# Re-timing a hand-planned instruction order: second mixer, stage openings, a fourth seven-product chunk

## The chip, the cores and the metric

One Trainium2 chip, one core. The metric is the device time of one execution in microseconds (us). The kernel before took 955.35 us (median of 3 runs, 955.19 to 955.69).

## The reference

A trunk of two layers on x (256 x 1024, float32). Each layer does

```
x = x + 0.5 * SwiGLU_1(rmsnorm(x))           # D_FF = 2816
h = rmsnorm(x); q_s|k_s|v_s|q_m = h @ W_in   # 1024 x 2560
self attention: layer 0 chunked with relative bias (12 heads),
                layer 1 differential with rotary, block-causal (6 heads)
memory attention: 4 heads into mem (256 x 1024)
x = x + concat(self, mem) @ W_out
x = x + 0.5 * SwiGLU_2(rmsnorm(x))
```

The differential attention of layer 1 norms each head of q and k (a power of -1/2), turns them by the rotary tables, takes two softmaxes a pair of heads, subtracts the second times lambda, and norms the result again.

## The kernel before, in words

**Products in three passes.** Every float32 weight and activation is split into a high part and a rest (`hi`, `lo`, both in the matrix engine's float32 format). One product is three matmuls of 512 columns: high by high (L511), high activation by low weight (L514), low activation by high weight (L517), all issued by the helper `dense`. ScalarE makes the high part (`split_hi`, L338), VectorE the rest (`split_lo`, L356).

**Stages.** For each layer: gate/up of FFN 1, down of FFN 1, the mixer, gate/up of FFN 2, down of FFN 2. Gate/up runs over 11 column groups g of 256 with two halves c of the contraction; two neighbouring groups are done with seven products in place of eight (`PAIR`). Down runs over 11 row chunks of 256. An ordinary down chunk is eight products. A chunk listed in `SEVEN` is seven: four sums of weight blocks are made on VectorE (L350) and four sums of activations (`seven_forms`, L681 to L694), and seven splits of the weights are made in place of four. The first such chunk of a stage takes two weight buffers; each later one ("guest") takes one and the two buffers of x's transposes, `xh` and `xl`, which are free in a down stage; the flag `xt_room` hands them from one guest to the next after the last product of the former. The last three down chunks are done output block by output block.

**The way of h.** After a gate/up group, `evac` makes h, writes it to DRAM (`hd`, L650) and reads it back turned (`hr`, L656), 3 us and then 2 us later by the plan. Four `hd` buffers rotate. The reads, the writes and all weight loads (L294, three raw buffers) go through one in-order queue, that of SyncE (SP).

**The order is written out by a planner.** `Flow` keeps a clock of its own while the program is built. Every step is a generator; it issues an instruction, adds the planned duration to its engine's time, and is taken up again when that time has come. The matrix engine's stream is issued by the main loop (`flow.pe`), the rest in between. So planned durations set only the order in each engine's queue; on the chip each engine runs its queue in order and waits on semaphores. Planned: 0.216 us a matmul, VectorE 0.07 + n/960, ScalarE 0.15 + n/1200, GpSimd as written at each call. `rsqrt` (L528) does the power on GpSimd (L532) with a planned 0.3 + 0.165 n us. The rotary step in `qk_evac` has two multiplications on GpSimd (L1259, planned 1.4 us together), one on VectorE (L1262) and their sum (L1266), before the transposes to the heads' layout (`qktp`, L525). In `attn_diff` the probabilities are transposed (`ptp`), multiplied with V (L1498), normed (L1512, L1514) and transposed again (`otp`).

**Stage openings.** `prep_half` transposes half of x's columns for one block of 128 rows, scales it (L557), makes `xh` on ScalarE (L560) and `xl` on VectorE (L562). Group 0 of every gate/up stage but the first goes row block by row block (`plain_chunk(0, c, (tb,))`), so that the first block's products run while the second block is prepared. `dense` waits for `xl` before its first pass.

## Time and profile before

| what | us |
|---|---|
| median of 3 runs | 955.35 |
| the profiled execution | 955.69 |
| its span, first to last instruction | 953.9 |
| PE busy (matmul) | 945.6 |
| VectorE busy | 820.0 |
| ScalarE busy | 587.0 |
| GpSimd busy | 109.1 |

In the profile PE is the matmul engine, DVE VectorE, ACT ScalarE, POOL GpSimd, SP SyncE; L and a number is a line of the kernel. Matmuls overlap in a pipeline, so that each shows a longer duration than the step from its start to the next one's start; it is the step that counts for the stream.

### The profile page before, as it was taken

Reading aid. Unit: us, or ns where it says so; the run is one execution under the profiler, and the core shown is the slowest. Engines: PE = TensorE matmul, PEld = TensorE weight load, DVE = VectorE, ACT = ScalarE, POOL = GpSimd, SP = SyncE. Lnnn points to the kernel's source line nnn. Section 1 sums busy time; section 2 is a strip of 40 time slices with the busy share of each in tenths; the row PEclk is TensorE's granted clock in tenths of the full one; section 3 lists DMA queues with packets and bytes.
Section 4 is the critical chain, followed back from the end, with each engine's and each line's share of the span. In section 5 each row is a group of like instructions: output and inputs, shape, how many; then the busy total and the mean of one; then the engine's idle time right before and its main releaser. Section 6 shows DMA issues by size and latency. Waiting matters only on the chain.

```text
span 953.9 us, 13334 instructions
## 1 busy us (share of the span) xinstructions
PE 945.6 (99%) x4475; PEld 774.1 (81%) x4475; DVE 820.0 (86%) x1483; ACT 587.0 (62%) x1121; POOL 109.1 (11%) x160
## 2 busy tenths in 40 slices
PE   9999999999999999999999999999999999999998
PEld 7888888887777888888888888888787778888886
DVE  7898978888777899979889899796999888999884
ACT  6556566677676746647546656564676865665650
POOL 1000057621210100000000000000434200000000
PEclk9999999999999999999999999999999999999999
DMA  8987799486525387887746679775641367588751
GB/s 265 289 263 236 224 354 296 158 276 210 177 90 177 97 266 225 262 287 219 245 146 219 208 226 288 247 253 166 196 158 57 121 214 228 183 275 276 239 197 45
DMA packets 169887, 204.04 MB, mean 214 GB/s; under 512 B 10137, under 2 KB 145114, under 8 KB 169818
## 3 DMA queue, kind: packets, MB, share of 16 engines
q1 hardware_dynamic: 169498, 202.78, 66.0%
q8 instruction: 35, 0.57, 0.3%
q10 hardware_dynamic: 320, 0.40, 0.1%
q14 instruction: 34, 0.28, 0.1%
HBM read 188.99 MB, written 14.16 MB: 213 GB/s over the span
## 4 chain that ended last, share of the span: by engine, by line
PE 90%; DVE 6%; DMA 2%; ACT 1%; issue 1%; SPq 0%; ACTq 0%; DVEq 0%
PE gu L517 13%; PE gu L514 13%; PE gu L511 13%; PE acc L511 9%; PE acc L517 9%; PE acc L514 9%; PE pair_m L511 3%; PE pair_m L514 3%; PE pair_m L517 3%; PE pj L517 2%; PE pj L511 2%; PE pj L514 2%; DVE lo L356 2%; PE S L1360 1%; DMA x<-in_x_dram 1%; PE AV L1441 1%
## 5 line engine op out<-in xcount | busy, mean ns | idle before, releaser
L338 ACT CAST hi<-raw 128x512 fp32r<-128x512 f32 (+1 forms) x467 | 336.3, 770 | 172.6 <-DMA raw<-in_ffn_w_up_dram 45.6
L356 DVE TENSOR_TENSOR lo<-raw,hi 128x512 fp32r<-128x512 f32 (+1 forms) x467 | 391.9, 875 | 35.5 <-ACT hi L338 35.4
L514 PE MATMUL gu<-lo,xh 128*128 128x512 f32 x576 | 224.7, 390 | 0.5 <-DVE lo L356 0.5
L517 PE MATMUL gu<-hi,xl 128*128 128x512 f32 x576 | 224.5, 390 | 0.4 <-DVE xl L562 0.4
L511 PE MATMUL gu<-hi,xh 128*128 128x512 f32 x576 | 224.4, 390 | 0.0
L517 PEld LDWEIGHTS gu<-hi,xl 128*128 128x128 f32 x576 | 108.1, 188 | 23.9 <-DVE xl L562 1.7
L514 PEld LDWEIGHTS gu<-lo,xh 128*128 128x128 f32 x576 | 108.1, 188 | 23.5 <-DVE lo L356 1.4
L511 PEld LDWEIGHTS gu<-hi,xh 128*128 128x128 f32 x576 | 108.2, 188 | 22.3
L517 PE MATMUL acc<-hi,ht 128*128 128x512 f32 x280 | 109.5, 391 | 0.0
L511 PE MATMUL acc<-hi,ht 128*128 128x512 f32 x280 | 109.2, 390 | 0.0
L514 PE MATMUL acc<-lo,ht 128*128 128x512 f32 x280 | 109.1, 390 | 0.0
L338 ACT CAST hi<-wsum 128x512 fp32r<-128x512 f32 x82 | 47.7, 619 | 26.5 <-DVE wsum L350 26.5
L514 PE MATMUL pj<-lo,xh 128*128 128x512 f32 x160 | 64.0, 400 | 0.0
L517 PE MATMUL pj<-hi,xl 128*128 128x512 f32 x160 | 63.8, 399 | 0.0
L511 PE MATMUL pj<-hi,xh 128*128 128x512 f32 x160 | 63.8, 399 | 0.0
L514 PEld LDWEIGHTS acc<-lo,ht 128*128 128x128 f32 x280 | 52.6, 188 | 10.9
L517 PEld LDWEIGHTS acc<-hi,ht 128*128 128x128 f32 x280 | 52.6, 188 | 10.8
L511 PEld LDWEIGHTS acc<-hi,ht 128*128 128x128 f32 x280 | 52.6, 188 | 10.7
L532 POOL TENSOR_TENSOR xr<-v,nhalf 128x1 f32<-128x1 f32 x12 | 10.3, 861 | 435.1 <-DVE v L530 435.1
L356 DVE TENSOR_TENSOR lo<-wsum,hi 128x512 fp32r<-128x512 f32 x82 | 52.8, 680 | 0.0
L633 ACT ACTIVATE sil<-gu,xr 128x256 f32<-128x256 f32 x72 | 33.7, 468 | 29.8 <-PE gu L517 29.7
L532 POOL TENSOR_TENSOR hf<-v,nhalf 128x8 f32<-128x8 f32 (+1 forms) x20 | 31.4, 1570 | 87.3 <-DVE v L530 78.9
(232 smaller groups left out, 1429.5 us busy)
## 6 DMA issues: line engine op xcount, KB each, us to landing
raw<-in_ffn_w_down_dram SPq DMA_DIRECT2D x176, 256.0 KB, 4.5
raw<-in_ffn_w_gate_dram SPq DMA_DIRECT2D x82, 512.0 KB, 4.0
raw<-in_ffn_w_up_dram SPq DMA_DIRECT2D x82, 512.0 KB, 5.4
raw<-in_w_in_dram SPq DMA_DIRECT2D x32, 512.0 KB, 4.4
hd<-hb SPq DMA_DIRECT2D x44, 256.0 KB, 4.6
hr<-hd SPq DMA_DIRECT2D x44, 256.0 KB, 4.6
raw<-in_w_out_dram SPq DMA_DIRECT2D x8, 1024.0 KB, 5.1
raw<-in_w_mem_kv_dram SPq DMA_DIRECT2D x4, 1024.0 KB, 5.3
```

The source lines that it names most:

```text
L338: nc.scalar.copy(out=it.part(0, q, w), in_=src())
L356: nc.vector.tensor_sub(it.part(1, q, w), src(), it.part(0, q, w).bitcast(F32))
L511: nc.tensor.matmul(out=ps, lhsT=xh, rhs=wh, start=start, stop=False)
L514: nc.tensor.matmul(out=ps, lhsT=xh, rhs=wl, start=False, stop=False)
L517: nc.tensor.matmul(out=ps, lhsT=xl, rhs=wh, start=False, stop=stop)
L532: nc.gpsimd.tensor_tensor(out=dst, in0=v[:, :n], in1=nhalf[:, :n], op=ALU.pow)
L633: nc.scalar.activation(sil, ps[tb][:, 0:256], AF.Silu, scale=xt.r[tb])
L1360: nc.tensor.matmul(out=ss[e][:, pr, :nk], lhsT=q[rows, pr, :], rhs=k[rows, pr, :], start=i == 0, stop=i == len(passes) - 1)
L1441: nc.tensor.matmul(out=av[64 * e:64 * e + 64, pr, :], lhsT=vsrc(kb, pr, e), rhs=pts[e][:, pr, kb, :], start=(kb == 0), stop=(kb == nb - 1))
```

## The change

The list of seven-product down chunks of the last stage goes from (1, 4, 7) to (1, 3, 5, 7). A new helper `two_phases` takes the place of `dense` where group 0 is done row block by row block: for four slices it issues the two passes with `xh`, then the four passes with `xl`; it waits first for the time of `xh` (kept in the new list `th`) and only then for that of `xl`. The planned time of the power on GpSimd becomes 0.5 + 0.17 n, that of the rotary multiplications 2.1. In `attn_diff` two steps are resumed 0.3 us later. The reading of h is issued 8 us in place of 2 us after the write's buffer is given back, for all groups but the last three.

```
-    SEVEN = {(0, 1): (), (0, 2): (1, 4, 7), (1, 1): (1, 4, 7), (1, 2): (1, 4, 7)}
+    SEVEN = {(0, 1): (), (0, 2): (1, 4, 7), (1, 1): (1, 4, 7), (1, 2): (1, 3, 5, 7)}
...
         nc.tensor.matmul(out=ps, lhsT=xl, rhs=wh, start=False, stop=stop)
+        used(c)
+        return flow.pe(T_MM)
+
+    def used(c):
         c.uses -= 1
         if c.uses == 0:
             hl_left[0] += c.n
             xt_room[0] |= c.guest
-        return flow.pe(T_MM)
+
+    def two_phases(ps, xt, tb, c, kks, start, stop):
+
+        for k, kk in enumerate(kks):
+            flow.until(lambda: c.lot[k] is not None and xt.th[tb][kk] is not None)
+            flow.at(max(xt.th[tb][kk], c.lot[k]))
+            at[0] = max(at[0], c.index)
+            for i, w in enumerate((c.part(0, k), c.part(1, k))):
+                nc.tensor.matmul(out=ps, lhsT=xt.h[tb][:, kk, :], rhs=w, start=start and k == i == 0, stop=False)
+                flow.pe(T_MM)
+                flow.step()
+        for k, kk in enumerate(kks):
+            flow.until(lambda: xt.t[tb][kk] is not None)
+            flow.at(xt.t[tb][kk])
+            nc.tensor.matmul(out=ps, lhsT=xt.l[tb][:, kk, :], rhs=c.part(0, k), start=False, stop=stop and kk == kks[-1])
+            used(c)
+            t = flow.pe(T_MM)
+            flow.step()
+        return t
...
-        yield flow.pool(0.3 + 0.165 * n)
+        yield flow.pool(0.5 + 0.17 * n)
...
         nc.scalar.copy(out=xt.h[tb][:, ks, :], in_=y)
-        yield flow.act(512)
+        t = flow.act(512)
+        xt.th[tb][ks] = [t] * 4
+        yield t
...
             g2.give()
-            yield flow.now + 2.0
+            yield flow.now + (8.0 if g < NG - 3 else 2.0)
             yield g2.has()
...
             for tb in tbs:
+                if len(tbs) == 1:
+                    t = two_phases(ps[tb], xt, tb, plan[l, nm, "gu"][g, c], range(4 * c, 4 * c + 4), c == 0, c == 1)
+                    if c == 1:
+                        end[tb] = t
+                    continue
...
                     flow.dve(512)
-                    yield flow.pool(1.4)
+                    yield flow.pool(2.1)
                     nc.vector.tensor_add(m1, m1, m2)
...
             pt, t = yield from p_transpose(e0, nk)
-            yield t
+            yield t + 0.3
...
             t = flow.dve(256)
             banks.give()
-            yield t
+            yield t + 0.3
             yield from o_transpose(o, tb, grp, gcs[:, 3:4])
```

## Rows read from the trace of the kernel before

**Rows 1.** The page: busy time of each engine, its share of the span, instructions.
```profile
PE 945.6 (99%) x4475; PEld 774.1 (81%) x4475; DVE 820.0 (86%) x1483; ACT 587.0 (62%) x1121; POOL 109.1 (11%) x160
```

**Rows 2.** Waits of PE, whole span: who waited for whom, us, times, longest.
```profile
PE qktp L525 <- DVE m L1266: 0.7, 2, 0.6
PE otp L525 <- DVE of L1512: 0.5, 1, 0.5
...
PE AV L1498 <- ACT PT L1374: 0.5, 1, 0.5
PE gu L517 <- DVE xl L562: 0.4, 1, 0.4
```

**Rows 3.** Windows (stretch, length; PE, PEld, DVE, ACT, POOL busy; clock): mixers, last down.
```profile
222.00:305.00 83.00, 83.00 (x515) 65.14 (x516) 65.24 (x179) 60.75 (x158) 11.45 (x7) 1.00 0.48 154
...
680.00:750.00 70.00, 68.03 (x373) 53.40 (x372) 65.39 (x147) 49.28 (x140) 28.49 (x24) 1.00 0.41 136
...
892.00:950.00 58.00, 58.00 (x257) 47.88 (x255) 43.88 (x77) 26.20 (x51) 0.00 (x0) 1.00 0.46 150
```

**Rows 4.** Timeline of PE, second mixer: start, duration, [idle before, releaser].
```profile
679.75 0.39 PE L517 MATMUL pj<-hi,xl 128*128 128x512 f32 x1
...
685.19 0.39 PE L517 MATMUL pj<-hi,xl 128*128 128x512 f32 x1
686.15 0.63 PE L525 MATMUL qktp<-ident,m 128*128 128x128 f32 x4 [0.57 <-DVE m L1266]
...
726.49 0.71 PE L1498 MATMUL AV<-V,PT 128*128 128x128 f32 x4 [0.45 <-ACT PT L1374]
...
745.23 0.41 PE L525 MATMUL otp<-ident,o 128*128 128x128 f32 x2 [0.49 <-DVE of L1512]
```

**Rows 5.** Groups of VectorE and ScalarE, 880 to 953 us: count, busy, mean ns.
```profile
L350 DVE TENSOR_TENSOR wsum<-raw,wsum 128x512 f32<-128x512 f32 x6 | 4.1, 686 | 0.1
...
L338 ACT CAST hi<-wsum 128x512 fp32r<-128x512 f32 x6 | 3.5, 617 | 0.0
```

**Rows 6.** Timeline, last down stage: PE's first matmul, VectorE, a weight load on SP.
```profile
892.26 0.39 PE L511 MATMUL acc<-hi,ht 128*128 128x512 f32 x1
...
913.18 0.28 DVE L681 TENSOR_TENSOR sf<-hr 128x128 f32<-128x128 f32 x1
...
916.58 0.68 DVE L694 TENSOR_TENSOR h<-sf,h 128x512 fp32r<-128x512 f32 x1
...
922.00 4.93 DVE L356 TENSOR_TENSOR lo<-raw,hi 128x512 fp32r<-128x512 f32 x8
...
919.70 2.53 SPq L294 DMA_DIRECT2D raw<-in_ffn_w_down_dram  x4
```

**Rows 7.** The page, DMA issues: KB each and median us from issue to landing.
```profile
raw<-in_ffn_w_down_dram SPq DMA_DIRECT2D x176, 256.0 KB, 4.5
```

**Rows 8.** Timeline of VectorE and PE at the opening of the last gate/up stage.
```profile
783.08 0.65 DVE L562 TENSOR_TENSOR xl<-y,xh 128x512 fp32r<-128x512 f32 x1
...
783.04 0.39 PE L514 MATMUL gu<-lo,xh 128*128 128x512 f32 x1
783.78 0.50 PE L517 MATMUL gu<-hi,xl 128*128 128x512 f32 x1 [0.35 <-DVE xl L562]
```

**Rows 9.** Waits of the SP queue, whole span: us, times, longest.
```profile
SPq L656 <- DMA hd<-hb: 50.1, 22, 4.7
```

**Rows 10.** Groups of GpSimd by shape, 660 to 790 us: count, busy, mean ns.
```profile
L1259 POOL TENSOR_TENSOR m<-qkn,ropeS 128x256 f32<-128x256 f32 x12 | 12.1, 1027 | 7.5 <-DVE qkn L925 4.7 <-ACT k L1022 1.8 <-PE pj L517 1.1
L532 POOL TENSOR_TENSOR hf<-v,nhalf 128x8 f32<-128x8 f32 x6 | 11.0, 1832 | 17.4 <-DVE v L530 9.1 <-DVE sst L583 8.3
L532 POOL TENSOR_TENSOR of<-v,nhalf 128x2 f32<-128x2 f32 x6 | 6.3, 1056 | 24.4 <-DVE v L530 24.4
```

**Rows 11.** Timeline of VectorE and GpSimd around one rotary multiplication.
```profile
681.19 1.23 DVE L1262 TENSOR_TENSOR m<-qkn,ropeC 128x512 f32<-128x512 f32 x1
...
680.89 2.12 POOL L1259 TENSOR_TENSOR m<-qkn,ropeS 128x256 f32<-128x256 f32 x2 [1.08 <-PE pj L517]
```

More of the change, by code (lines that the diff above doesn't have):

```diff
@@ L541, in __init__ @@
             self.r = [sm.tile([P, 1], F32, tag="xr", name="xr", bufs=4) for _ in range(2)]
-            self.t = [[None] * KT for _ in range(2)]
+            self.t, self.th = ([[None] * KT for _ in range(2)] for _ in range(2))
             self.rt = [None, None]
```

## The prediction

> **What bounds the kernel.** I read the page first. PE is busy for 945.6 of 953.9 us [rows 1], at the full granted clock in every window read (1.00, the 2.4 GHz level, [rows 3]), so the matmul stream is the limit and only two things can change the time: fewer matmuls, or fewer holes in the stream. How large the holes are the busy share does not tell. Therefore the list of PE's waits came second [rows 2], the windows by stage third [rows 3], and the timeline at each hole last [rows 4]. Apart from the first 13 us, which the change leaves alone, the trace has holes in two places: the second mixer, where PE lacks 70.00 - 68.03 = 1.97 us between 680 and 750, and the opening of the last gate/up stage, where it waits 0.4 us for `xl`. Mixer 1 and the last down stage have none [rows 3].
>
> The reader should see what a hole really costs. In a full stream one matmul of 512 columns starts 0.227 us after the other: 24 steps from 679.75 to 685.19 are 5.44 us [rows 4]. The transpose at 686.15 starts 0.96 us after the matmul before it, 0.73 late, though the profile calls 0.57 of this idle. So each hole costs about 0.16 us above its idle time, since the overlap of neighbours is lost too. The mixer's idle time is spread over seven holes; the three largest are in the group, the other four share 1.97 - 1.51 = 0.46 us. The loss is 1.97 + 7 x 0.16 = 3.1 us.
>
> **The change, part by part.**
>
> *The fourth seven-product chunk.* The list goes from three entries to four, so one product, three matmuls, falls away: 3 x 0.227 = 0.68 us of the stream. What it adds lies beside the stream: four more weight sums (0.69 us alone, [rows 5]) and three more splits on VectorE, in a row some 0.61 us each (8 splits in 4.93 us, [rows 6]), 4.3 us; three more casts of 0.62 us on ScalarE, which is busy 26 of 58 us; and the activation sums with their splits, 2.3 us of VectorE (four at 0.2 us and 1.5 us of splits, the last of 0.68; the one chunk in the group spreads them from 913.18 to 917.3 between weight work). VectorE has 58.00 - 43.88 = 14.1 us to spare in this stage [rows 3], so these 6.6 us fit as a total. What matters is when. A guest's splits may begin only after the last product of the guest before it, and guests stand two chunks apart now, not three. With the down stage starting at 892.26 [rows 6] and 0.68 us a product, chunk 3 ends at 912.66; chunk 5 runs from 918.10 to 922.86, chunk 7 from 928.30 to 933.06. Chunk 5's seven splits are through at about 912.7 + 0.9 + 4.3 = 917.9 (0.9: the first cast and 0.3 for hand-overs), and its third product, which uses the seventh split, comes at 919.5. Chunk 7's are through at 922.9 + 0.9 + 4.3 = 928.1, needed at 929.7. The margin is 1.6 us both times. Chunk 10's load, issued at 919.70 now, waits for chunk 7's three plain splits, until about 925.5; 2.5 us of issuing and 4.5 us to the landing of a piece [rows 6, 7] make 932.5 at the latest; cast and split by 934; needed at 933.06 + 4 x 0.68 = 935.8. I take no stall: -0.68 us. Bounds: -0.68, and +2.3 if the activation sums of chunks 5 and 7 (4.6 us), which the plan lets begin at chunk 3, fall wholly into chunk 5's splits: its third product is then 3.0 us late.
>
> *The openings.* Group 0 waits for `xl` at 783.78, 0.74 us after the matmul before it, so 0.51 us late, with one step 0.11 too long behind it: 0.62 us [rows 8]. With the passes of `xh` first, six other matmuls, 1.4 us, come ahead of the first that needs `xl`, more than the 0.5 missing; `xh` was there in time before. -0.62 us. The two other openings have no hole and gain nothing; the count of matmuls and weight loads is the same. Next to be late would be `xh` itself, made one VectorE step earlier. Bounds -0.62 and 0.
>
> *h read later.* Nothing on PE waits for h or for a weight's landing [rows 2], so both signs are hidden. It spares SP up to 50.1 us of standing at a read whose write has not landed, 22 times, with weight loads queued behind it [rows 9]; those loads were not late for PE either. On the other side h comes 6 us later for groups 0 to 7; the latest of these, group 7, still has three gate/up groups of 48 matmuls (10.9 us each) before the down stage begins. If that cover were gone, a late chunk would cost its whole lateness. I take 0; bounds ±0.3, half of one hole.
>
> *Planned times.* They move no work, only places in the queues. A power of eight values is planned at 1.62 us and measures 1.83; the pair of rotary multiplications 1.4 against 2 x 1.03 = 2.06; the power of two values 0.63 against 1.06 [rows 10]. So the planner puts the sum (L1266) and the transposes behind it too early: VectorE and then PE stand at an instruction whose input is not there, and what is queued behind stands too, weight splits on VectorE and projection matmuls on PE. After the change the planned chain up to `qktp` is 0.24 + 0.7 = 0.94 us longer; the holes at `qktp` are all smaller (0.73 the largest). The chain to `otp` gains 0.3 + 0.2 + 0.3 = 0.8 against a hole of 0.65. `AV` gains 0.3 against 0.61 with its idle 0.45, so 0.3 stays; one hole at `ptp` after the softmax gets no margin of its own and I leave it, 0.3. For new holes that a shuffled order opens I take 0.3. Gain 3.1 - 0.3 - 0.3 - 0.3 = 2.2 us. Bounds: -3.1 (all gone) and 0. VectorE has 4.6 us free in that window [rows 3], enough. Mixer 1 gets the longer power as well; it has no holes, its VectorE is busy only 65 of 83 us [rows 3], and later planning loosens it: 0.
>
> The sum: -0.68 - 0.62 - 2.2 = -3.5 us. From the profiled execution's 955.69 that is 952.2; the median stands 0.34 below it, so **951.9 us**.
>
> **A rule against the fixed numbers.** In the trace the VectorE multiplication that runs beside GpSimd's two takes 1.23 us [rows 11], where a two-input subtraction of the same size takes 0.68 with GpSimd idle [rows 6]: they hold each other up by 0.55 us. So neither duration is a constant that a planner can know. The Trainium skill, page "SBUF — State Buffer", section "SBUF: two separate sides", says why: GpSimd shares a port pair with VectorE instructions that read two SBUF inputs, as "an exclusive lock, not a bandwidth split", and the loser waits out the whole instruction. The measured 0.55 fits such a lock. What the behaviour would make of the time is rival 1.
>
> **The rivals.**
> 1. *Half of the holes come back at other places.* The new order sets other VectorE instructions beside GpSimd's; each of the six rotary steps costs 0.55 us somewhere, 3.3 us in all, and the holes return in part. For it: [rows 11], and VectorE busy 93% of this window. Against it: the new 2.1 already holds the shared time (2.06). Mixer gain about 0.9: 955.35 - 0.68 - 0.62 - 0.9 = 953.1 us. Chance 0.22.
> 2. *The last stage pays.* Chunk 5 or 7 stalls by up to the bound, 3.0 us; say 2: 951.9 + 2 = 953.9. For it: margins of 1.6 us only. Against: PE runs 5% slower than planned (0.227 to 0.216) and VectorE as planned, so a place that is free in the plan is freer on the chip. Chance 0.10.
> 3. *Slower.* In the second mixer the gap that the longer rotary step opens in VectorE's plan is filled with a weight split (0.6 to 0.7 us), which on the chip runs late and stands before the sum that the transposes wait for. One such split at all six chains is 4.2 us, with the old holes kept: 955.35 - 1.3 + 4.2 = 958.2. From two chains on (1.4 us) it outweighs the other gains, and from five (3.5 us) the kernel is slower by over 0.2%. For it: VectorE's 93%. Against it: the planner puts a split only where it sees VectorE free. Chance 0.08.
> 4. *The re-planning does nothing on balance*, and only the dropped product and the opening show: 955.35 - 1.3 = 954.05. Chance 0.06.
>
> The forecast, 951.0 to 953.0, has 0.54.
>
> **How the numbers follow.** On the good side the bounds of the terms add to 955.35 - 4.4 = 950.9, with 0.3 for h 950.6. On the other side the range takes in rivals 1, 2 and 4 up to 954.8 and leaves out rival 3 and the worst of 2, some 0.12 together. 0.2% is 1.9 us, about what a measurement of this kernel can tell from no change; faster by more means under 953.44. That is all of the forecast, two thirds of rival 1 and a little of rival 2: 0.54 + 0.15 + 0.03 = 0.72. Slower by more is most of rival 3, 0.07. The rest, 0.21, is within.
>
> **What would show it.** In the changed kernel's trace PE's waits name no `xl`; PE's idle time in the second mixer's 70 us is below 0.8 in place of 1.97; the last down stage has 84 products in place of 85, 57.1 us, and no hole; L656 does not stand on `hd`. The prediction is wrong if PE waits for `lo` after 912 us (rival 2), if the mixer's holes remain under other names (rivals 1, 4) or grow behind L356 (rival 3).

## The result, and the profile after

The changed kernel takes **958.86 us** (median of 22 runs, 955.34 to 961.42) where the kernel before, run between them, takes 955.53 (22 runs, 954.45 to 956.77): a ratio of 1.0030, with a 95% interval of 1.0022 to 1.0039. It is slower by 3.3 us; the prediction said 951.9 and a range up to 954.8. **It was wrong, in sign and in size.**

The profiled run of the changed kernel took 961.42, the slowest of its 22, so its rows show 2.6 us more loss than the median has. In ten of the 22 runs the mean granted clock is 0.996 to 0.998 and the median time 960.3, in the other twelve it is 0.999 or 1.0 and the median 957.1. Stage by stage, from the first matmul of a stage to the first of the next in PE's timeline (us):

| stage | before | after | difference | predicted |
|---|---|---|---|---|
| to the first matmul | 7.13 | 7.30 | +0.17 | 0 |
| FFN 1 of layer 0, memory's K and V | 204.49 | 205.58 | +1.09 | 0 |
| mixer 1 | 103.65 | 103.32 | -0.33 | 0 |
| FFN 2 of layer 0, FFN 1 of layer 1 | 353.36 | 353.36 | 0 | 0 |
| mixer 2, projections | 70.95 | 68.49 | -2.46 | -2.2 for |
| mixer 2, output products | 34.60 | 40.45 | **+5.85** | the mixer |
| last gate/up | 118.08 | 117.43 | -0.65 | -0.62 |
| last down | 57.57 | 59.30 | **+1.73** | -0.68 |
| last matmul to the span's end | 4.07 | 4.38 | +0.31 | 0 |

The sum is 5.71, the difference of the spans (959.6 - 953.9). Two gains look right almost to the digit, and two stages lose what nobody priced. Of the -2.46 some 0.2 is only moved: two transposes more, at steps of 0.11 us, come behind the first output product (362 instructions of PE stand before it in the kernel before, 360 after). How much of the rest is gain is worked out below. The 1.09 is mostly the landing of x at the start, which varies from run to run (PE waits 0.3 us for x in the profile before and 1.3 here).

The page's busy line of the changed kernel answers to [rows 1]: three matmuls fewer, thirteen VectorE instructions more, and PE "busy" 2.2 us longer.

```profile
PE 947.8 (99%) x4472; PEld 776.0 (81%) x4472; DVE 825.1 (86%) x1496; ACT 589.9 (61%) x1126; POOL 108.0 (11%) x160
```

Fewer matmuls that are busy for longer: the windows below show a stretch at the lower clock, which the busy share hides. PE's waits over the whole span [rows 2] name new waits, and `xl` no longer:

```profile
PE S L1389 <- ACT PT L1403: 2.0, 2, 1.8
PE acc L514 <- DVE lo L356: 1.8, 2, 1.0
...
PE qktp L547 <- DVE m L1295: 0.2, 1, 0.2
```

The windows of [rows 3], same stretches and columns:

```profile
222.00:305.00 83.00, 82.99 (x512) 65.53 (x511) 65.50 (x180) 62.34 (x160) 11.46 (x7) 1.00 0.48 155
680.00:750.00 70.00, 69.41 (x381) 54.86 (x379) 65.35 (x147) 49.72 (x141) 27.79 (x25) 1.00 0.42 133
892.00:950.00 58.00, 56.17 (x247) 45.89 (x246) 52.96 (x99) 32.96 (x64) 0.00 (x0) 1.00 0.49 159
```

In the second mixer's first 70 us PE now lacks 0.59 us in place of 1.97. The last down stage, which had no hole, lacks 1.83, and VectorE works 9.1 us more there (8.4 when both windows are laid from the stage's first matmul; in e1 below, with the fourth chunk alone, 4.9).

**The opening** of the last gate/up stage went as said. VectorE and PE in the timeline, where `xl` of the second block [rows 8] is made:

```profile
785.65 0.68 DVE L586 TENSOR_TENSOR xl<-y,xh 128x512 fp32r<-128x512 f32 x1
...
785.77 0.39 PE L534 MATMUL gu<-hi,xh 128*128 128x512 f32 x1
786.00 0.39 PE L534 MATMUL gu<-lo,xh 128*128 128x512 f32 x1
786.23 1.07 PE L540 MATMUL gu<-hi,xl 128*128 128x512 f32 x4
```

PE works at passes with `xh` while `xl` is made, and no step there is longer than 0.23. But `xl` also comes sooner: 7.14 us after the stage's first matmul (785.65 - 778.51) in place of 8.90 (783.08 - 774.18). The experiments show that this would have closed the hole without the new passes.

**The second mixer's end.** The timeline from 745 to 761 us: the first chunk's load for the last gate/up, ScalarE, and PE.

```profile
745.98 0.37 SPq L294 DMA_DIRECT2D raw<-in_ffn_w_gate_dram  x1
746.39 1.23 SPq L294 DMA_DIRECT2D raw<-in_ffn_w_up_dram  x1
...
752.31 1.04 ACT L338 CAST hi<-raw 128x1024 fp32r<-128x1024 f32 x1 [2.10 <-DMA raw<-in_ffn_w_up_dram]
753.26 0.58 ACT L1403 COPY PT<-ptp 128x512 f32<-128x512 f32 x1
...
751.46 0.62 PE L1389 MATMUL S<-km,qmT 64*128 64x256 f32 x3
753.89 1.64 PE L1389 MATMUL S<-km,qmT 64*128 64x256 f32 x9 [1.81 <-ACT PT L1403]
...
759.47 0.63 PE L514 MATMUL acc<-lo,oT 128*128 128x512 f32 x1
759.90 0.63 PE L517 MATMUL acc<-hi,oT 128*128 128x512 f32 x1
```

ScalarE stands 2.10 us at the cast of a weight that has not landed. What PE waits for, a copy of 0.58 us (`PT`), is queued behind that cast. So the chain is load, cast, copy, PE; the page names only its last link. Then the clock goes. The windows (columns as in [rows 3]; the clock is the third number from the end):

```profile
750.00:753.00 3.00, 2.08 (x12) 1.37 (x10) 1.92 (x4) 0.90 (x2) 0.00 (x0) 1.00 0.37 129
753.00:755.00 2.00, 1.11 (x8) 1.11 (x9) 0.04 (x1) 2.00 (x8) 0.00 (x0) 0.66 0.00 0
755.00:757.00 2.00, 2.00 (x8) 1.58 (x8) 1.97 (x6) 1.60 (x5) 0.00 (x0) 0.50 0.00 0
757.00:759.00 2.00, 2.00 (x9) 1.85 (x9) 1.12 (x3) 0.48 (x3) 0.00 (x0) 0.50 0.00 0
759.00:761.00 2.00, 2.00 (x7) 1.58 (x6) 1.53 (x4) 2.00 (x9) 1.07 (x1) 0.63 0.72 193
761.00:763.00 2.00, 2.00 (x15) 1.69 (x14) 1.93 (x8) 0.98 (x4) 0.00 (x0) 1.00 0.96 329
```

From about 753.6 to 760.5 us the clock is 0.5, the 1.2 GHz level, and the stream shows PE fully busy at steps of 0.43 us in place of 0.227. In the kernel before the same twelve scores take 1.27 us, 0.106 each:

```profile
751.52 1.32 PE L1360 MATMUL S<-km,qmT 64*128 64x256 f32 x12
752.79 1.16 PE L1498 MATMUL AV<-V,PT 128*128 128x128 f32 x8
```

So the fourth, due at 751.78, is 2.1 us late; half of the 6.6 us that PE then works at the lower clock is 3.3. Together they are 5.4 of the 5.85.

In the kernel before the same load was issued 3.0 us earlier (2.1 when counted from the mixer's first matmul) and the cast waited for nothing but its buffer:

```profile
742.94 0.37 SPq L294 DMA_DIRECT2D raw<-in_ffn_w_gate_dram  x1
...
749.33 2.00 ACT L338 CAST hi<-raw 128x1024 fp32r<-128x1024 f32 x2 [0.82 <-PE acc L517]
```

**The last down stage.** Timeline of the changed kernel: the reads of h, ScalarE, VectorE, PE.

```profile
889.11 0.93 SPq L680 DMA_DIRECT2D hr<-hd  x2
...
893.67 0.62 ACT L689 CAST ht<-hr 128x512 fp32r<-128x512 f32 x1 [6.40 <-DMA hr<-hd]
...
894.33 0.69 DVE L691 TENSOR_TENSOR ht<-hr,ht 128x512 fp32r<-128x512 f32 x1 [5.26 <-ACT ht L689]
...
895.54 0.28 DVE L705 TENSOR_TENSOR sf<-hr 128x128 f32<-128x128 f32 x1
...
940.71 0.50 PE L514 MATMUL acc<-lo,ht 128*128 128x512 f32 x1 [0.87 <-DVE lo L356]
...
942.63 0.50 PE L514 MATMUL acc<-lo,ht 128*128 128x512 f32 x1 [0.96 <-DVE lo L356]
```

In the kernel before, the reads that meet here, the eighth and ninth of the eleven, were issued at 880.30 and 883.51. Now two go together at 889.11 and 889.53. Group 3 is half of the pair, whose products are spread between those of groups 5 to 8, so that it ends after group 7. By the plan's order the first of the two reads is group 8's, which stands at its own write, and group 3's, 8 us late, is queued behind it. ScalarE stands 6.40 us at the cast of group 8's h and VectorE 5.26 behind it. The stand alone is not the loss: with three chunks it was 3.61 and 1.71 us at these two groups in the kernel before, and 9.15 in e13 below, and the stage took 57.57 both times. Group 3 is in the new list, so its activation sums and splits come on top, from 895.54 on; counted from the stage's first matmul that is 8.2 us later than in e1, which reads h early (883.59). VectorE has that idle time taken from the middle of its work and is short of it at the end: from 900 to 940 us it is busy 39.7 of 40 (39.0 in e1).

```profile
930.00:940.00 10.00, 9.84 (x44) 7.82 (x42) 9.88 (x18) 7.09 (x14) 0.00 (x0) 1.00 0.52 164
```

The raw buffers come free only behind VectorE's splits, so the load of the last chunk is issued 35.4 us into the stage (32.1 in e1), and ScalarE stands for it:

```profile
937.43 0.63 ACT L338 CAST hi<-raw 128x512 fp32r<-128x512 f32 x1 [2.07 <-DMA raw<-in_ffn_w_down_dram]
```

That cast begins 41.5 us into the stage, 38.3 in e1. The splits of the last chunk come late, and PE waits twice.

### The profile page after: what moved, and what is told of

It reads as the page before. It is cut to its first block, busy times and chain, and to the rows that moved or that the text cites. A ratio compares the mean times of both kernels' runs of the same rounds, so it can differ in the third digit from the quotient of the medians.

```text
span 959.6 us, 13333 instructions
## 1 busy us (share of the span) xinstructions
PE 947.8 (99%) x4472; PEld 776.0 (81%) x4472; DVE 825.1 (86%) x1496; ACT 589.9 (61%) x1126; POOL 108.0 (11%) x160
## 4 chain that ended last, share of the span: by engine, by line
PE 70%; DVE 14%; DMA 9%; ACT 3%; issue 2%; SPq 2%; DVEq 0%; ACTq 0%
PE gu L514 8%; PE gu L517 8%; PE gu L511 8%; PE acc L517 7%; PE acc L511 7%; PE acc L514 7%; DVE lo L356 7%; DMA raw<-in_ffn_w_up_dram 5%; PE pj L517 2%; PE gu L534 2%; PE pj L511 2%; PE pj L514 2%; DVE wsum L350 2%; PE pair_m L514 2%; PE pair_m L511 2%
## 5 line engine op out<-in xcount | busy, mean ns | idle before, releaser
L338 ACT CAST hi<-raw 128x512 fp32r<-128x512 f32 (+1 forms) x466 | 335.0, 770 | 158.4 <-DMA raw<-in_ffn_w_up_dram 58.5
L514 PE MATMUL gu<-lo,xh 128*128 128x512 f32 x528 | 205.9, 390 | 0.5 <-DVE lo L356 0.5
L517 PE MATMUL gu<-hi,xl 128*128 128x512 f32 x528 | 205.6, 389 | 0.0
L511 PE MATMUL gu<-hi,xh 128*128 128x512 f32 x528 | 205.6, 389 | 0.0
L514 PEld LDWEIGHTS gu<-lo,xh 128*128 128x128 f32 x528 | 99.1, 188 | 21.8 <-DVE lo L356 1.4
L517 PEld LDWEIGHTS gu<-hi,xl 128*128 128x128 f32 x528 | 99.1, 188 | 20.9 <-DVE xl L586 0.5
L511 PEld LDWEIGHTS gu<-hi,xh 128*128 128x128 f32 x528 | 99.1, 188 | 20.5
L514 PE MATMUL acc<-lo,ht 128*128 128x512 f32 x272 | 106.2, 391 | 1.8 <-DVE lo L356 1.8
L517 PE MATMUL acc<-hi,ht 128*128 128x512 f32 x272 | 106.4, 391 | 0.0
L511 PE MATMUL acc<-hi,ht 128*128 128x512 f32 x272 | 106.2, 390 | 0.0
L511 PEld LDWEIGHTS acc<-hi,ht 128*128 128x128 f32 x272 | 51.1, 188 | 10.4
L517 PEld LDWEIGHTS acc<-hi,ht 128*128 128x128 f32 x272 | 51.1, 188 | 10.4
```

Source lines behind the costliest of these rows:

```text
L338: nc.scalar.copy(out=it.part(0, q, w), in_=src())
L511: nc.tensor.matmul(out=ps, lhsT=xh, rhs=wh, start=start, stop=False)
L514: nc.tensor.matmul(out=ps, lhsT=xh, rhs=wl, start=False, stop=False)
L517: nc.tensor.matmul(out=ps, lhsT=xl, rhs=wh, start=False, stop=stop)
```

## The experiments

Times are medians; each ratio is to the runs of the kernel before on the same chip, with its 95% interval. "Stage" numbers are steps between first matmuls, from one profiled run each.

### One part alone

Each of the four is the kernel before with one part of the change.

```
-    SEVEN = {..., (1, 2): (1, 4, 7)}
+    SEVEN = {..., (1, 2): (1, 3, 5, 7)}
```

> Only the list of the last down stage is changed, to (1, 3, 5, 7). Theory A (each part has its own fault): chunk 10's weights land too late even alone, since chunk 7 holds its raw buffer longer; PE waits twice for lo in the last 20 us, together 1 to 2.2 us, against 0.68 us saved, so the time is 956 to 957.2, and the second mixer is as before (1.97 us idle). Rival B (the late reading of h shifts the SP queue and makes both the late load and the stand in the mixer): no wait for lo at the end, 954.9.

Measured: 955.32, 0.9993 [0.9983, 1.0003]. The last down stage is 56.89 us, 84 products of 0.677, and PE waits for nothing in it. The predicted -0.68 is right for this part alone, and theory A's two waits are not there. VectorE is nearly as full as after, with 0.84 us free in the window that had 0.12 in the changed kernel:

```profile
930.00:940.00 10.00, 10.00 (x46) 8.29 (x45) 9.16 (x15) 2.67 (x5) 0.00 (x0) 1.00 0.08 28
```

The second: `two_phases`, `used` and `th` alone.

```
+                if len(tbs) == 1:
+                    t = two_phases(ps[tb], xt, tb, plan[l, nm, "gu"][g, c], ...)
```

> Only the openings are changed (passes of x's high part first). Theory A: PE's wait for xl of 0.4 us goes and nothing comes; about 954.9. Rival C (a new order in the openings shifts everything behind it, the second mixer too): another set of holes in the mixer, 954 to 957, and the wait for xl gone all the same.

Measured: 955.86, 0.9997 [0.9985, 1.0009]; the last gate/up is 117.43 as in the changed kernel, so the 0.65 is there in its stage, though the median, with an interval of 1.2 us to either side, can't show it.

The third: the planned times and the two 0.3 us.

```
-        yield flow.pool(0.3 + 0.165 * n)
+        yield flow.pool(0.5 + 0.17 * n)
...
-                    yield flow.pool(1.4)
+                    yield flow.pool(2.1)
...
-            yield t
+            yield t + 0.3
```

> Only the planned times are changed (power on GpSimd, rotary step, 0.3 us twice). Theory A: this is where the changed kernel's stand of 1.8 us comes from, ScalarE standing at a weight cast whose load has not landed, the transposed probabilities behind it, PE behind these, and then the granted clock at 0.5 for 6.8 us: time spread over 955 to 960 from run to run, median above 957. Rival B: no such stand; the holes of 1.97 us idle fall below 0.8 and the time is about 953.2.

Measured: 957.71, 1.0022 [1.0010, 1.0035]. The part that was to bring most loses 2 us. The second mixer's projections fall to 69.20, but the first mixer's rise to 72.50, with a hole of 1 us at the probabilities' transposes, where the kernel before has none, and the second mixer's output products to 36.34, with a wait of 0.7 us for the same copy `PT` as after. So theory A's stand is there, but at 0.7 and not 1.8, and in the profiled run the clock did not fall. The last gate/up takes 117.43, without the new openings.

The fourth: h read later.

```
-            yield flow.now + 2.0
+            yield flow.now + (8.0 if g < NG - 3 else 2.0)
```

> Only the reading of h is issued later. Theory A: no hole comes or goes, 955.4 within 0.3. Rival B: the SP queue's new order makes late loads in the second mixer (ScalarE waits there for a weight's landing) or at the last chunk, 956 to 960.

Measured: 957.05, 1.0010 [1.0000, 1.0020]. The interval ends at no change, so a loss is likely but not shown; the profile (955.21, the fastest of its runs) shows little of it: the first down stage takes 61.71 in place of 61.28, with a wait of 0.2 us of the transposes for x (L606) that the kernel before hasn't.

### All but one part, and the openings with the fourth chunk

```
-            yield flow.now + (8.0 if g < NG - 3 else 2.0)
+            yield flow.now + 2.0
```

> The changed kernel with h read as early as before. Theory A2 (the late reading of h moves group 3's activation sums, 2.3 us of VectorE, and the casts of h into the start of the last down stage, where four seven-product chunks leave VectorE no room, so that chunk 10 comes late): no wait of PE for lo after 912 us, VectorE idle less than 2 us in its longest wait for a cast of h; 1 to 3 us faster than the changed kernel's 958.9, so 956 to 958, since the mixer's stand remains. Rival (the fourth chunk alone is too much): the wait for lo at the end stays at 1 to 2 us and the time stays within 1 us of 958.9.

Measured: 955.90, 1.0005 [0.9992, 1.0018], 3.0 us under the changed kernel. The last down stage is back at 56.89. The first mixer's projections take 74.93, with the hole at the probabilities again. The mixer's stand, which was to remain, is smaller: the output products take 36.30, the cast stands 0.94 us in place of 2.10, and PE's longest wait for `PT` is 0.7 in place of 1.8:

```profile
PE S L1389 <- ACT PT L1403: 0.9, 2, 0.7
```

```
-        yield flow.pool(0.5 + 0.17 * n)
+        yield flow.pool(0.3 + 0.165 * n)
```

and so with the 2.1 and the two 0.3:

> The changed kernel with the planned times of before. Theory A2: the second mixer has its old holes (about 1.2 to 2 us idle) and no stand of over 1 us, the clock stays at 1.00 in it; the wait for lo at the end stays, 1 to 2 us; median 956 to 957, top of the runs below 959. Rival (the late reading of h or the new openings make the mixer's stand): medians near 958.9 and runs of 960 and more as in the changed kernel.

Measured: 957.87, 1.0021 [1.0010, 1.0033]. That is 0.9 over the 957 named. The second mixer's output products are at 34.63, with no fall of the clock; the last down stage is 59.64. ScalarE stands at the same cast:

```profile
889.41 0.62 ACT L689 CAST ht<-hr 128x512 fp32r<-128x512 f32 x1 [6.33 <-DMA hr<-hd]
```

So the two losses part: the mixer's needs the times, the last stage's the late reading with the fourth chunk. But the mixer's is not the times' alone. With them and h read early (e3, e5) the cast begins 4.8 us after the issue of its load's second half, stands 1.00 and 0.94, and PE waits 0.7; with them and h read late (the changed kernel, e10) it begins 5.9 us after, stands 2.10 and 2.07, and PE waits 1.8. Why the same load lands 1.1 us later there, no run shows.

The fourth chunk and the openings together (the diffs of e1 and e2), twice:

> The two parts that lost nothing alone, together: four seven-product chunks and the openings with the high part first. If they add: 0.68 + 0.62 us below the kernel before, 954.2 against 955.5, mixer as before. If the new order of the openings spoils the last stage: PE waits for lo there and the time is 955 to 957.

> The same kernel as in the run of seven products and openings, for a second profile: its runs fell into two groups, 953.2 to 954.6 and 955.8 to 957.4, and the first profile was of the lower group. Theory F (the upper group has a hole of 2 us in mixer 1, at the first transposed probabilities, where ScalarE stands at the memory keys that come back from DRAM): if this profile is of the upper group, mixer 1's projections take 73 to 74 us in place of 71.4. Rival: the two groups differ before 13 us, in the landing of x.

Measured: 955.78, 0.9996 [0.9984, 1.0007], and 955.70, 0.9995 [0.9985, 1.0006]. The first kernel's twelve runs lie in two groups, 953.2 to 954.6 and 955.8 to 957.4. Its profile, 953.71, is of the lower group: last gate/up 117.43, last down 57.39. The second profile, 955.75, shows no hole in the first mixer, which had been suspected. It has small ones in several places (0.6 in two at `qktp` in the second mixer, 0.6 in two at `lo` in the last stage, the landing of x); of the 2.1 us between the two spans 1.0 is the second mixer and 0.7 the last down stage, 58.10. What puts a run into either group is not settled. Nor is the fourth chunk safe here, with h read early: ScalarE stands 7.3 and 7.5 us at group 3's h at the start of the last down stage, PE waits for `lo`, and 57.39 and 58.10 are over the 56.89 of e1.

### The second mixer's stand

```
-LAT = 1.5
+LAT = 3.1
```

> The changed kernel with the planner's time from the end of a weight load's transfer to its landing at 3.1 in place of 1.5 us, so that a load is planned at 6.0 us in all, about what the trace shows (745.98 to 752.2). Theory D (ScalarE and VectorE stand at weight casts whose load has not landed, ahead of the attention's small steps): ScalarE's waits for landing weights in the second mixer fall below 0.5 us, the stand of 1.8 us and the low clock go, 954 to 956. Rival (it is VectorE's and GpSimd's crowding, not the landings): holes of the same sum elsewhere in the mixer, 958 to 960.

Measured: 955.62, 1.0001 [0.9992, 1.0010]: with every load planned to land 1.6 us later the stand is gone (output products 35.25), but the whole order shifts, and there are holes of 1.3 in the first mixer and 0.8 in the last stage.

So the same for one load alone, in the changed kernel:

```
-            c.arrive = dma_free[0] + LAT
+            c.arrive = dma_free[0] + LAT + (2.0 if c is plan[1, 2, "gu"][0, 0].raws[0] else 0.0)
```

> The changed kernel; only the first weight chunk of the last gate/up stage is planned to land 2 us later, so that its casts on ScalarE come behind the transposed probabilities and the exponentials of the memory heads and not ahead of them. Theory E (this one cast makes PE's stand of 1.8 us, and the stand makes the low clock): the stretch from the first output product of mixer 2 to the first gate/up product goes from 40.5 to about 35 us, the clock stays at 1.00 there, no run of 960 or more, median 956 to 957; the last down stage keeps its 59.3 us. Rival (the crowding of the second mixer makes the hole anyway, at another instruction): 958 to 959.5.

Measured: 955.87, 0.9997 [0.9988, 1.0005]. One planned landing time takes 3.0 us off the changed kernel's median (3.4 when each is set against the kernel before of its own session). The output products take 35.28, the clock stays at 1.00. Its mean is 0.999 or more in all 11 runs, as in the 18 of e11 and e16 below, which have the same edit; in e10, which keeps the stand, it is 0.998 in 5 of 12. The last down stage keeps its loss (58.67).

### The last stage's stall

```
-            yield flow.now + (8.0 if g < NG - 3 else 2.0)
+            yield flow.now + (8.0 if g < NG - 3 and (l, nm) != (1, 2) else 2.0)
```

> The changed kernel; only in the last FFN h is read as early as before. Theory A2 (late h and the fourth chunk together): the last down stage falls from 59.3 to 56.9 us and PE does not wait for lo there; mixer 2 as in the changed kernel, runs of 960 stay possible but 2.4 us lower; median 956.5. Rival (the late reading costs in earlier stages): last stage shorter, the median moves by less than 1 us.

Measured: 957.04, 1.0005 [0.9996, 1.0013], 1.8 us under the changed kernel (2.2 by the sessions' own kernels before). The last down stage is 56.89, and ScalarE's stand at h has shrunk:

```profile
889.58 0.62 ACT L689 CAST ht<-hr 128x512 fp32r<-128x512 f32 x1 [0.96 <-DMA hr<-hd]
```

The stand in the second mixer is still in this run, as long as in the changed kernel, but its clock stayed up. PE's timeline and the window behind it:

```profile
755.38 0.97 PE L1389 MATMUL S<-km,qmT 64*128 64x256 f32 x9 [1.79 <-ACT PT L1403]
```

```profile
756.00:758.00 2.00, 2.00 (x16) 1.73 (x15) 1.91 (x6) 2.00 (x7) 0.00 (x0) 1.00 0.00 0
```

That prices the two halves: the whole mixer took 106.27 us here, 108.94 in the changed kernel's profile, so 2.7 us were the clock's in that run (3.0 by the output products, 37.43 and 40.45).

The fourth chunk and the late reading with nothing else (the diffs of e1 and e4):

> Of the change the fourth seven-product chunk and the late reading of h, both openings and times as before. Theory L: these two together make the stall of the last down stage. That stage takes 58.5 to 59.7 in place of 56.89 with the fourth chunk alone and 57.57 with three; PE waits about 2 us for lo after 930, and ScalarE stands over 5 us at a cast of h near 890. Rival: the openings or the times have a part in it; then the stage stays at 57.6 or less. Time by theory L 957 to 958, by the rival 955 to 956.5.

Measured: 956.98, 1.0009 [1.0000, 1.0018]. The last down stage takes 58.18, over the 56.89 of the fourth chunk alone, with one wait for `lo` of 0.9 in place of two; ScalarE's stand is 3.86. So the pair makes a stall by itself, smaller than expected: 58.5 to 59.7 and waits of 2 us had been named. With the openings as well (e6) it was 59.64; how much of the rest is theirs and how much the running's, two profiles don't tell.

### Which planned time costs what

Only the power (the diff of e6 turned round, on the kernel before):

> Of the change only the power's planned time (0.5 + 0.17 n). Theory M: this is what makes the first mixer's hole, since the first mixer has no rotary step: the order of ScalarE from the memory's norm on differs, the table load stands before the first exponentials, PE waits 0.9 us or more for pe at the probabilities' transposes near 233, and the first mixer's projections take 72.3 or more in place of 71.1 to 71.6. The second mixer's projections gain under half of the 2.46, so 69.8 or more. Rival: the hole there is chance of the running, as large with the rotary time alone; then this run shows 71.6 or less and no table load near 230. Time by theory M 955.5 to 957, by the rival 954.5 to 955.5.

Measured: 957.96, 1.0015 [1.0006, 1.0024], 1.0 over the range named. The first mixer's projections take 74.71. ScalarE, VectorE and PE in the timeline:

```profile
189.09 0.20 ACT L1195 ACTIVATE le<-le 128x2 f32<-128x2 f32 x1
...
189.92 1.28 ACT L1157 ACT_TABLE_LOAD   x1
191.21 0.26 ACT L1157 ACTIVATE ropew<-ropew 128x64 f32<-128x64 f32 x1
...
229.47 0.51 ACT L1068 ACTIVATE km<-kr,gcol 128x256 fp32r<-128x256 f32 x1 [2.56 <-DMA kr<-kd]
230.00 1.28 ACT L1408 ACT_TABLE_LOAD   x1
231.29 0.40 ACT L1408 ACTIVATE pe<-pe,nm 128x128 f32<-128x128 f32 x1
...
233.58 0.88 DVE L1422 TENSOR_SCALAR pe<-pe,rs 128x128 f32<-128x128 f32 x4
...
233.93 0.52 PE L525 MATMUL ptp<-flip,pe 128*128 128x128 f32 x2 [1.86 <-DVE pe L1422]
```

and the same places before:

```profile
189.10 1.28 ACT L1157 ACT_TABLE_LOAD   x1
190.40 0.26 ACT L1157 ACTIVATE ropew<-ropew 128x64 f32<-128x64 f32 x1
...
190.82 1.28 ACT L1195 ACT_TABLE_LOAD   x1
192.11 0.21 ACT L1195 ACTIVATE le<-le 128x2 f32<-128x2 f32 x1
...
228.77 0.51 ACT L1068 ACTIVATE km<-kr,gcol 128x256 fp32r<-128x256 f32 x1 [2.24 <-DMA kr<-kd]
229.19 0.38 ACT L1408 ACTIVATE pe<-pe,nm 128x128 f32<-128x128 f32 x1
```

This effect is well hidden. Before, the two sines of the rotary tables (L1157) come first and the exponential of two numbers for lambda (L1195) second; that one brings the exponentials' table back, at 190.82, where nobody waits. With the longer power the planner sets lambda first. The sines now have the last word, and the table is loaded again at 230.00, inside the chain from the memory's K to the first softmax, at whose start ScalarE stands 2.56 us anyway. Of the chain's delay at the first exponential, 231.29 to 229.19 before, 1.28 is the load and 0.70 a later landing of K; PE waits 1.86. Behind the hole the clock was 0.87, 0.50 and 0.78 in the windows of 2 us from 234 to 240, which makes 3.4 us at 0.5. Four kernels have a table load near 230 (e3, e5, e7, e13), with waits of PE of 0.98 to 2.09 behind it; the others have none, and at most 0.90.

The Trainium skill, page "ScalarE: Activation LUTs", section "What ACT_TABLE_LOAD costs", gives about 1283 ns for the load, and the trace agrees (1.28). It adds about 1380 ns of draining; the rows don't show that here, since the load starts 0.02 us after the instruction before it ends, and the exponential 0.01 us after the load.

Only the rotary multiplications (1.4 to 2.1):

> Of the change only the rotary multiplications' planned time (2.1). Theory M: the first mixer has no such step, so it stays at 71.0 to 71.6 with no hole over 0.3 us; the second mixer's projections take most of the gain, 68.5 to 69.5 in place of 70.95, and the out-products that follow keep 34.6 or rise to 36 where the first load of the last gate/up lands after ScalarE's cast has its turn. Rival: the gain comes from the power's time and the 0.3 steps, and the projections stay over 70. Time by theory M 953 to 954.5, by the rival 955 to 956.

Measured: 955.05, 0.9986 [0.9977, 0.9995]: this number alone is a gain, but smaller than expected and not where it was expected. Nothing of it lies in the first mixer (72.11, with a wait of 0.6 us at the same place for a K that landed late, and no table load), and the second mixer's projections, 69.87, are what e2, e4 and e8 have with the old time (69.80 to 69.85). The second mixer as a whole took 104.08 us against 105.55, and the last gate/up 117.43: with the old openings its hole of 0.65 is gone.

### Both mended, and the losing numbers left out

The diffs of e9 and e10 together, on the changed kernel, in two sessions:

> Both of these edits together. If the two faults are all that spoils the change: 951.9 + 0.5 for the start, so 952 to 953.5, faster than the kernel before by 2 to 3 us. If mixer 1 has a fault of its own (the hole of 1 to 2 us at the transposes that other kernels with the new planned times show): 953.5 to 955.5, spread over the runs.

> The kernel changed in two places (the first cast of the last gate/up planned 2 us later, h read 2 us after in the last FFN) a second time. If it is the faster one: median 953.5 to 954.5, 0.997 to 0.999 of the kernel before, its last down stage 56.9, its last mixer's out-products 34.6 to 35.4 with no wait of PE over 1 us. If the first result was luck of seven runs: 955 to 956.

Measured: 953.94 (7 runs), 0.9980 [0.9968, 0.9991], and 954.08 (11 runs), 0.9979 [0.9969, 0.9989]. Both causes together are worth 4.8 to 4.9 us of the changed kernel's median, as 3.0 and 1.8 add to; by the sessions' own kernels before they are worth 5.0 to 5.3, and 3.4 and 2.2 add to 5.6. The 952 to 953.5 of the first expectation is missed: the first down stage, where h is still read late, takes 62.6 and 62.5 us in place of 61.3.

The changed kernel without the longer power and the late reading (its other parts kept):

> The changed kernel without its two parts that lost time alone: the power's planned time as before, h read early as before. Kept are the fourth seven-product chunk, the openings, the rotary time and the 0.3 us steps. Theory: every part kept gains alone or with the others (0.68 + 0.65 + about 1.1 in the second mixer), the first mixer has no table load near 230: last gate/up 117.43, last down 56.9 to 57.5, second mixer's projections 69 to 70, out-products 34.2 to 35.5; 953 to 954.3. Rival: the rotary time alone moves the first cast of the last gate/up before its load's landing too, then the out-products show 36 or more and the time is 955 to 956.

Measured: 953.72, 0.9978 [0.9965, 0.9990]. Every stage is in the range named: no table load near 230, last gate/up 117.43, last down 56.89, the second mixer 69.32 and 35.27.

And with the power planned longer in the second mixer alone, h read early, the first cast planned 2 us later (e9's diff):

```
-        yield flow.pool(0.5 + 0.17 * n)
+        yield flow.pool(0.5 + 0.17 * n if flow.now > 500.0 else 0.3 + 0.165 * n)
```

> The changed kernel with h read early as before, the first cast of the last gate/up planned 2 us later, and the longer power planned in layer 1 alone. If the power's time loses by the order it sets in the first layer and gains in the second: first mixer as before (71.0 to 72.1, no table load near 230), second mixer's projections 68.0 to 68.8, out-products 34.6 to 35.4, last gate/up 117.4, last down 56.9; 952.3 to 953.8, so below the kernel mended in two places only (953.94 and 954.08). If the power's time harms the second mixer as well: projections over 69 or out-products over 36, and 954.5 or more.

Measured: **953.02** (12 runs, 952.33 to 955.51), 0.9975 [0.9963, 0.9986], the lowest median of the study, though the intervals of e11, e16 and e17 overlap with it. Its stages: mixer 1's projections 71.05, mixer 2's 69.15 and 35.30, last gate/up 117.44, last down 56.89. The projections missed their 68.8, so that the longer power gains in the second mixer is not shown. PE's waits, of the whole span, behind the first 13 us:

```profile
PE qktp L547 <- DVE m L1295: 0.8, 1, 0.8
...
PE S L1389 <- ACT PT L1403: 0.2, 1, 0.2
```

## Why the prediction was wrong

**The bound was read rightly**: PE's stream, and the holes in it. All that was gained or lost is holes and three matmuls, as [rows 1 to 3] said, but for one thing: behind a hole the clock may fall, and in the profile 2.1 us of hole were followed by 3.3 lost to the clock.

**The fourth chunk**, -0.68: right by itself (56.89 in e1, e5, e10, e11 and e16 to e18). The margins held there; with the openings and the old times they did not quite (57.39 and 58.10, e8 and e12). The sums that were feared in chunk 5's splits are not what failed.

**The openings**, -0.62: right in size, 0.65 in every kernel that has them, and by the mechanism named in e2. But it is not theirs alone: e3, e13 and e14, with the old openings and new planned times, have 117.43 as well, since `xl` comes 7.1 to 7.8 us after the stage's first matmul and not 8.9. In the changed kernel either part would have closed the hole.

**"h read later: I take 0; bounds ±0.3"** is the first step that failed. The cover was taken as "the latest of these, group 7, still has three gate/up groups" before the down stage. The latest is group 3: the pair's products are strewn between the others, and in the timeline its last ones end at 868.73, 27 us before the down stage (895.93) and not 33. Its read then falls behind another group's in the queue, and the fourth chunk needs just this group's sums. What gave way is the margin of chunk 10, for which the prediction had a split by 934 and a need at 935.8, 41.7 and 43.5 us into the stage: in the changed kernel the split ends at 44.7 (940.65 - 895.93). Two parts priced one by one, at -0.68 and 0, are worth +1.73 together in the profile; undoing one of them in the last FFN gives back 1.8 to 2.2 us of the median. Of the 50.1 us that SP stood at reads [rows 9] the waits of its queue still show a third:

```profile
SPq L680 <- DMA hd<-hb: 17.9, 5, 5.1
```

That those stands cost nothing before was right, and so removing them could bring nothing. In the first down stage the late reading costs 0.4 to 1.3 us in six of its kernels' profiles (61.65 to 62.61 in e4, e6, e9 to e11 and e16, where the kernels without it have 61.27) and nothing in the changed kernel's own, in e7 and in e15.

**"Planned times: -2.2, bounds -3.1 and 0"** is the second, and the costlier. Three things were wrong in it.
- *The upper bound.* "They move no work, only places in the queues" was taken to mean that nothing can be lost. The places are what can be lost: a cast moved ahead of its load's landing stood 2.10 us with a softmax's copy behind it, and a table load moved by 40 us cost 1.28 in a chain. Rival 3 had this kind of loss (an instruction filled in before one that PE waits for) at 0.08, with a weight split on VectorE; it came on ScalarE, whose queue holds casts of weights that depend on DMAs, and which the prediction did not look at in the mixers. With the times alone the stand was 0.7 us of PE (e3); to 1.8 it grew only with h read late (the changed kernel, e10).
- *Mixer 1 at 0*, "later planning loosens it". Alone, the longer power costs 3.3 us there (74.71 against 71.37, e13). In the changed kernel as a whole the late reading happens to put lambda back behind the sines (table loads at 188.59 and 191.34; without it, in e5, the second is at 230.31), and mixer 1 lost nothing. That the table above has 0 there is luck.
- *The gain.* From the second mixer's first matmul to the last gate/up's, the kernels with the planned times of before took 104.40 to 105.77, mean 105.07 (before, e1, e2, e4, e6, e8, e12, e15); those with all of them in the second mixer, and no stand of 1.8, 103.32 to 105.54, mean 104.19 (e3, e5, e7, e9, e11, e16, e18; e3 and e5 have the stand of 0.7). The gain is 0.9 us, 1.2 without e3 and e5, so about half of the 2.2. The profile before, with 105.55, was on the high side of its kind: part of its 3.1 us of holes was that run's own. One and the same kernel took 104.40 in e8 and 105.42 in e12. So the -2.46 of the table, so near the forecast, is in good part luck.

With this the sum can be made again: -0.68 - 0.65 - 1.0 = -2.3 where no stand comes in between, and e18 measured 953.02 - 955.57 = -2.55 (interval -3.5 to -1.3). In the changed kernel the stand with its clock is worth 3.4 (e9) and the stall 2.2 (e10), each set against the kernel before of its session. On top of e16's 954.08 - 955.77 = -1.7 they make +3.9, where +3.3 was measured, within the noise of four medians.

**The rivals.** Rival 2 named the sign of one loss (PE waits for `lo` after 912) and about its size, but put it at chunk 5 or 7, by activation sums that come too early; they came late, and chunk 10 paid. Rival 1's mechanism, the shared port of VectorE and GpSimd, no run parted from the rest. Both tests of the prediction that named a wait for `xl` and the number of products came true; the one for the mixer (idle below 0.8 in its 70 us) came true as well, at 0.59, and misled: the loss lay 2 us behind that stretch. Two failed: the last down stage has a hole, and the reads of h still stand on `hd` five times (17.9 us).

**Open.** Why the same stand lowers the clock in one run and not in another (the changed kernel and e10); what parts the two groups of e8's runs; why the load lands later where h is read late; and whether the openings and the fourth chunk, which show in their stages, show in the medians of e1, e2, e8 and e12, whose intervals hold the full gain as well as none.

## What to carry to other kernels

In an order written by a planner a "measured" duration is not a correction with one sign: it re-sorts every in-order queue, so list, for each engine, the instructions that change places and look for three kinds among them, a cast ahead of its load's landing, a table switch, and a read queued behind another's write. Price edits that share a buffer or a group together, and find the covered distance in the timeline, not from the group's number. When one part wins and another loses, mend the one place (a planned landing 2 us later was worth 3.0 to 3.4 us) before the whole is given up.

## What the runs showed of the hardware

- One stand of PE of 1.8 us in a stream otherwise full was followed by 6.8 us at a granted clock of 0.5 (windows above), those of 1.9 in e13 and 2.1 in e5 by 3.4 us each; another of 1.8 (e10) by none.
- The second half of a pair of weight loads, issued at 746.39, landed 5.8 us later (its median on the page is 5.1); the same pair, issued 3 us earlier in the kernel before, was there before its cast had its turn.
- The write of the memory's K to DRAM and its reading back take from 218.05 to 229.47 in e13, 11.4 us, and ScalarE stands 0.7 to 2.8 us at its end in the twenty profiles, 2.24 in the kernel before.
